# Four modulation groups of the second layer, moved from the first layer's mixers to the end of its experts

## The chip, the cores and the metric

The kernel runs on one core of one Trainium2 chip. The metric is the device time of one execution in microseconds; three runs of the kernel before are shown. The engines are named as the profile names them: PE (matmul; PEld is its weight load), DVE (vector), ACT (scalar), POOL (GpSimd) and SP (the sync engine, which here issues nearly all DMAs; its rows read SPq).

## What is computed

Two layers of a transformer trunk over 512 latent and 256 context tokens of 1024 values. In each layer a vector of six modulations, made of a conditioning vector and a weight, scales and shifts the normed tokens; four token mixers run side by side (a gated recurrence HGRN2, neighbourhood attention, a gated linear attention, latent attention); an output projection follows, and then a mixture of 32 experts with two experts for each token. Cut to what matters here:

```python
for layer in range(DEPTH):
    m_lat = jnp.split((c_act @ w_mod[layer] + b_mod[layer])[:, None, :], 6, axis=-1)
    m_ctx = jnp.split(c_ctx_act @ w_mod[layer] + b_mod[layer], 6, axis=-1)
    h = rmsnorm(x, norm1_g[layer]) * (1.0 + m_lat[1]) + m_lat[0]
    hc = rmsnorm(xc, norm1_g[layer]) * (1.0 + m_ctx[1]) + m_ctx[0]
    p = split_projection(h @ w_in[layer])
    ...
    x = x + m_lat[5] * y[b * l_ctx:].reshape(b, n, D_MODEL)
```

`w_mod[layer]` is 1024 x 6144. The kernel cuts its columns into 12 groups of 512. Groups 0 to 3 are `m[0]` and `m[1]`, the shift and scale of the first norm; a layer needs them at its very start. They depend on nothing that the layer before computes.

## The kernel before, in words

**Modulation.** `modulation` (L323) is a generator; one step makes one group. It loads the bias into one of four small tiles `bmt` (L329, two DMAs), loads the weight in two DMAs of 1 MB into ring tiles (L334), runs 32 matmuls on PE with the 32-column conditioning `cT` as the stationary side (L336, recorded at the helper's line L294; the trace has two instructions for each), adds the bias on DVE into `mr` (L338), and for groups 0 to 3 turns the result on PE (L340) and copies it into `ABs`, the scale and shift of the first norm (L341, L346).

**The last mixers of a layer** (L1424). `weave` (L428) takes steps from three generators so that their progress stays in proportion to the numbers in `STEPS` (L38): HGRN2 (66), latent attention (72), and `mods` (12 in the first layer, 8 in the second). In the first layer `mods` makes groups 4 to 11 of its own layer and then groups 0 to 3 of the next (L1419 to L1422). The weights of `mods` go through a ring of two tiles (L1413). The profile's first layer has this stage from about 345 to 506 us.

**Experts.** For each of 16 pairs of experts six pieces of 1 MB are loaded (128 + 64 DMAs in both layers, L1453 and L1458) into 18 slots that `wslot` (L1441) hands out in turn, so that a piece reuses the slot of the piece 18 before it, that is, of the third pair before. Each load also waits until the load four before it has landed (`DEEP`, L34). Pair `p_` runs on PE: up (L1917), activation, down (L1939); DVE weights the result, and POOL adds it to the stream `XA` in DRAM with an indirect DMA (`scatter`, L1992). A run-time branch (L2018) adds work for pairs with many tokens. After the pairs stands one more branch (L2032) for the rare case of many tokens left; it is not taken here. Its other arm waits, on SP, for every DMA that SP has issued, and on PE for PE's own work; only behind it stand the instructions of the next layer. The first layer's experts run from about 620 to 921 us.

**Start of the next layer.** SP loads 0.5 MB of `w_in` in three DMAs of short rows (L514) and then six token tiles `xn` from `XA` (L463), which wait for the last scatter. ACT splits the weight (L519) and squares each `xn` (L471), DVE scales it (L479), PE turns it (L490), ACT applies `ABs` (L497), and the projections begin.

**What sets the order.** Each engine runs its instructions in one fixed order, made at build time by a scheduler from the order of the code, with loads moved ahead where only a free tile holds them back. Semaphores hold an instruction until its inputs and its tile are free; whatever stands behind a waiting instruction on its engine waits too.

Of the kernel before, what the change touches and what calls it, by code (L numbers as in the profile page):

```python
# [17 lines left out]
P = 128  # L18
# [7 lines left out]
NEXP = 32  # L26
# [8 lines left out]
YE = 3  # L35
PRE = 2

STEPS = ((38, 24, 60, 18, 12, 12, 66, 72, 12), (38, 24, 60, 18, 12, 12, 66, 72, 8))  # L38
NWM = 4
NU, NX, NM = 25, 8, 8  # L40
TOKS = ((256, 512), (0, 256))
# [45 lines left out]
def hybrid_kernel(ctx: ExitStack, tc: tile.TileContext, a: dict, out: bass.AP, dbg=None, stop=None):  # L87
    nc = tc.nc
# [79 lines left out]
    def pmd():  # L168
        return psum("md")[:, 0:P]
# [123 lines left out]
    def mm(o, lhsT, rhs, start, stop, **kw):  # L293
        TE.matmul(o, lhsT, rhs, start=start, stop=stop, **kw)  # L294
# [24 lines left out]
    bmt = [cp.tile([P, P], F32, name=f"bmt{i}") for i in range(4)]  # L319
    for t_ in bmt:  # L320
        V.memset(t_, 0.0)

    def modulation(L, gs, slot=None, bank=None):  # L323

        for i_, g in enumerate(gs):
            cs = slice(g * 512, (g + 1) * 512)
            bt = bmt[i_ % 4]
            for w in range(2):
                nc.sync.dma_start(bt.rearrange("(j r) c -> j r c", r=32)[:, w, :], a["b_mod"][L, cs].rearrange("(j c) -> j c", j=4))  # L329
            pm = bank()[:, 0:P] if bank else pmd()  # L330
            for k in range(KT):
                if k % 4 == 0:
                    wt = (slot or ring)([P, 4, 512])
                    nc.sync.dma_start(wt, a["w_mod"][L, k * P:(k + 4) * P, cs].rearrange("(k p) c -> p k c", p=P))  # L334
                for j in range(4):
                    mm(pm[32 * j:32 * j + 32, 0:P], cT[:, k, :], wt[:, k % 4, j * P:(j + 1) * P], k == 0, k == KT - 1)  # L336
            mr = cp.tile([P, P], F32, name="mr", tag="mr", bufs=2)
            V.tensor_tensor(mr, pm[:, 0:P], bt, op=ALU.add)  # L338
            if g < 4:
                TE.transpose(pm[:, 0:P], mr, ident)  # L340
                V.tensor_copy(ABs[L][:, :, g // 2, 4 * (g % 2):4 * (g % 2) + 4],  # L341
                              pm[:, 0:P].rearrange("p (j c) -> p c j", j=4)[:, 0:2, :])
            if g in (2, 3):
                ks = slice(4 * g - 8, 4 * g - 4)
                for w in range(2):
                    V.scalar_tensor_tensor(ABs[L][:, w, 1, ks], ABs[L][:, w, 1, ks], 1.0, g1s[:, L, ks], op0=ALU.add, op1=ALU.mult)  # L346
            if g in (8, 9):
                g2 = cp.tile([P, P], F32, name="g2", tag="g2", bufs=1)
                V.memset(g2, 0.0)
                for w in range(2):  # L350
                    nc.sync.dma_start(g2.rearrange("(j r) c -> j r c", r=32)[:, w, :],
                                      a["norm2_g"][L, (g - 8) * 512:(g - 7) * 512].rearrange("(j c) -> j c", j=4))
                V.scalar_tensor_tensor(mr, mr, 1.0, g2, op0=ALU.add, op1=ALU.mult)
            if 6 <= g < 10:
                TE.transpose(pm[:, 0:P], mr, ident)
                V.tensor_copy(AB2s[L][:, :, g // 2 - 3, 4 * (g % 2):4 * (g % 2) + 4],
                              pm[:, 0:P].rearrange("p (j c) -> p c j", j=4)[:, 0:2, :])
            if g >= 4:
                for w in range(2):
                    nc.sync.dma_start(MOD[L][w, cs].rearrange("(j c) -> j c", j=4),  # L360
                                      mr.rearrange("(j r) c -> j r c", r=32)[:, w, :])
            yield
# [18 lines left out]
    def layer(L):  # L381
        last = L == DEPTH - 1
# [40 lines left out]
        def drain(*gens):  # L423
            for g_ in gens:
                for _ in g_:
                    pass

        def weave(*gens):  # L428

            st_ = [[g_, 0, n_] for g_, n_ in gens]  # L430
            while st_:
                s_ = min(st_, key=lambda e_: e_[1] / e_[2])
                try:
                    next(s_[0])
                    s_[1] += 1
                except StopIteration:
                    st_.remove(s_)
# [454 lines left out]
        def gla_values(E, gv):  # L892
            wt = wchunk([(C_G + 256, 256)], not E.safe)
            gv.extend(v_tiles(E))
            yield from tm(E, wt, 0, 256, lambda p, n: S.copy(gv[n], p), range(NT))
# [504 lines left out]
        nq, nk, nv, hq, hg, gg, zz, gs, hv, gqk, gv, cs, mw, mr_ = ([] for _ in range(14))  # L1400
        gqk.extend((gq, gk))
        drain(gla_values(Ex, gv))
        st = STEPS[L]
        weave((gla(E, gqk, gv, c2, False), st[0]),
# [13 lines left out]

        def mods():  # L1419
            yield from modulation(L, range(4, 12))  # L1420
            if not last:
                yield from modulation(L + 1, range(4))  # L1422

        weave((hgrn_, st[6]),  # L1424
              (chain(mla_qkv(Em, hu, cs, c2, mw, mr_), restore(Ex), mla(Em, mr_)), st[7]), (mods(), st[8]))
# [13 lines left out]
        NW = sum(SLOTS[L])  # L1439

        def wslot():  # L1441
            i = pieces[0] % NW
            pieces[0] += 1
            for p_, n_ in slots:
                if i < n_:
                    return wpools[p_].tile([P, 2048], F32, name=f"w{p_}", tag=f"w{p_}", bufs=n_ + XGS * (p_ == 2))
                i -= n_
# [21 lines left out]
        def prefetch(n, order=True, after=None):  # L1469

            for _ in range(n):
                e, i = len(loaded) // 6 + NEXP // 2 * (len(loaded) % 2), len(loaded) % 6 // 2
                if len(loaded) < 3 * NEXP:
                    loaded.append(expert_part(wgu[e], wdn[e], i, order, after, True))
# [19 lines left out]
        def split_chunk(raw):  # L1494
            hi = ring([P, 4, 256], F32R)
            S.activation(hi, raw, AF.Copy)
            lo = ring([P, 4, 256], F32R)
            V.tensor_tensor(lo, raw, hi.bitcast(F32), op=ALU.subtract)  # L1498
            return hi, lo
# [7 lines left out]
        wt = split_chunk(raw)  # L1507
# [151 lines left out]
        for c in range(4):  # L1659
# [3 lines left out]
            for kh in range(2):  # L1663
                if (c, kh) != (0, 0):
                    wt = split_chunk(raw)
# [168 lines left out]
        def rows(p_):  # L1834
            if p_ < NEXP // 2:
                return gather(xgs[p_ % NG], tab(0, p_, "row"))
# [9 lines left out]
        def tab(b, p_, n_):  # L1846
            return tabs[b][n_][:, p_:p_ + 1] if n_ in tabs[b] else None
# [54 lines left out]
        def block_in(xg, xT=None):  # L1902
# [8 lines left out]
                (V.tensor_copy if g else S.copy)(xT[:, 4 * g:4 * g + 4], pt.rearrange("p (k t) -> p k t", k=4))  # L1911
            return xT

        def span(hv):
            return slice(64 * hv[0], 64 * hv[-1] + 64)

        def block_up(w_, xT, hv=(0, 1)):  # L1917

            pm = pmm()
            for k in range(KT):  # L1920
                for h in hv:
                    hs = span([h])
                    mm(pm[hs, :], xT[:, k, hs], w_[h][k // 4][:, k % 4, :], k == 0, k == KT - 1)
            ac = wk.tile([P, 256], F32, name="ac", tag="ac", bufs=1)
            rs_ = span(hv)
            S.activation(ac[rs_], pm[rs_, 0:256], AF.Silu)  # L1926
            V.tensor_tensor(ac[rs_], ac[rs_], pm[rs_, 256:512], op=ALU.mult)  # L1927
            return ac
# [63 lines left out]
        def scatter(ye, row):  # L1992


            G.indirect_dma_start(out=XA, out_offset=bass.IndirectOffsetOnAxis(ap=row, axis=0), in_=ye, in_offset=None,  # L1995
                                 bounds_check=T - 1, oob_is_err=False, compute_op=ALU.add)
# [3 lines left out]
        def pair(p_):  # L2000
            return [loaded[6 * p_ + h:6 * p_ + 6:2] for h in range(2)] if p_ >= 0 else None
# [6 lines left out]
        xT = into(0)  # L2008
        for p_ in range(NP):
            prefetch(max(0, min(6 * p_ + NW, 3 * NEXP) - len(loaded)), False)  # L2010
            w_ = pair(p_)
            xT_, ac = xT, block_up(w_, xT)
            rows(p_ + NG)
            if p_ + 1 < NP:
                xT = into(p_ + 1)
            gt = gates_of(tab(0, p_, "own"))
            ye = weighted(p_, block_down(w_, block_act(ac)), gt, tab(0, p_, "gws"))
            with tc.If(cregs[p_] > 0):  # L2018
                with tc.If(cregs[p_] < 2) as c1_:
                    half_swapped(p_, w_[0], xT_, ye, gt, 1)  # L2020
                with c1_.Else():
                    with tc.If(cregs[p_] < 3) as c2_:
                        half_swapped(p_, w_[1], xT_, ye, gt, 0)
                    with c2_.Else():
                        swapped(p_, w_, xT_, ye, gt)

                        gather(yes[:, (p_ + 2) % YE], tab(1, p_, "row"))
                        y1 = block_down(w_, block_act(block_up(w_, into(p_, 1, xT_))))
                        scatter(weighted(p_ + 1, y1, gates_of(tab(1, p_, "own")), tab(1, p_, "gws")), tab(1, p_, "row"))
            scatter(ye, tab(0, p_, "row"))  # L2030

        with tc.If(cregs[NP] > 64):  # L2032
            for b in range(2, 12):
# [87 lines left out]
```

## Time and profile before

| what | value |
| --- | --- |
| three runs, median (lowest to highest) | 1757.4 us (1752.9 to 1762.54) |
| profiled execution, own time | 1761.22 us |
| its span, first to last instruction | 1759.4 us |
| mean granted PE clock | 0.933 |
| PE busy, whole span | 1463.9 us (83%) |
| DVE, ACT, POOL busy | 711.2, 525.2, 348.3 us |
| loads of `w_mod` in the ring | 40 of 1 MB |
| loads of expert weights | 192 of 1 MB |
| moved by all DMA engines | 366.01 MB |

The profile cuts the span into 40 slices of 44 us and gives busy shares in tenths. Whole-span shares mix stages of different limits, so the stretches around the change are read one by one: the last mixers of the first layer, the end of its experts, and the first 30 us of the second layer.

### The profile page before, as it was taken

The page shows a single profiled execution, that of the slowest core. Times are in us where ns is not written, and L with a number is a line of the kernel's source. Part 1 is how long each engine was busy: PE and PEld are TensorE (multiplying, and loading weights), DVE is VectorE, ACT ScalarE, POOL GpSimd, SP SyncE. Part 2 cuts the span into 40 slices and gives each one's busy share as a digit, 9 for nine tenths or more (in the row PEclk, how much of TensorE's full clock was granted, in tenths as well). Part 3 has the DMA queues.
Part 4 walks back from the last instruction along what each step waited for, and adds up shares of the span by engine and source line. Part 5 has one row for each costly group of instructions (what it writes and reads, how often), then busy time and mean ns, then how long its engine had stood idle before and what let it go on. Part 6 is the DMA issues. An engine that isn't in the chain of part 4 may idle for free. (4 is left out here: it accounts for less than half of the span.)

```text
span 1759.4 us, 26653 instructions
## 1 busy us (share of the span) xinstructions
PE 1463.9 (83%) x10515; PEld 986.2 (56%) x10515; DVE 711.2 (40%) x1427; ACT 525.2 (30%) x1067; POOL 348.3 (20%) x263
## 2 busy tenths in 40 slices
PE   6999999989889748887876999897887866888883
PEld 4888778746679723322236888685455852322221
DVE  5263353586733552111125443626874262111111
ACT  5342453464422101100006433626543211000001
POOL 0021120120101333645330120302110131111100
PEclk9999989999999869999997999899898888999997
DMA  9232311167447299999974333104343659999995
GB/s 329 88 110 75 115 56 34 39 226 239 160 159 214 107 393 354 383 372 383 375 274 130 107 101 90 31 31 134 109 140 128 187 183 382 378 361 364 374 387 220
DMA packets 179800, 366.01 MB, mean 208 GB/s; under 512 B 39608, under 2 KB 90496, under 8 KB 179328
## 3 DMA queue, kind: packets, MB, share of 16 engines
q1 hardware_dynamic: 170288, 342.10, 54.8%
q0 software_dynamic: 9216, 20.99, 4.7%
q8 instruction: 138, 2.26, 0.5%
q14 instruction: 78, 0.64, 0.1%
q10 hardware_dynamic: 80, 0.02, 0.0%
HBM read 338.48 MB, written 39.65 MB: 215 GB/s over the span
## 5 line engine op out<-in xcount | busy, mean ns | idle before, releaser
L294 PE MATMUL mm<-w,xT 128*64 128x512 f32 (+1 forms) x1120 | 273.4, 597 | 34.8 <-DMA w<-in_moe_w_gu_dram 16.3
L294 PE MATMUL pj<-h,w 128*128 128x256 f32 (+1 forms) x1224 | 228.0, 341 | 0.5 <-DVE u L935 0.3
L294 PEld LDWEIGHTS pj<-h,w 128*128 128x128 f32 x1224 | 189.5, 191 | 29.1 <-issue 5.2
L294 PEld LDWEIGHTS mm<-w,xT 128*64 128x64 f32 x1120 | 88.3, 141 | 192.0 <-issue 137.6
L294 PE MATMUL sc<-w,aT 128*64 128x512 f32 x536 | 138.4, 607 | 19.3 <-ACT aT L1936 16.7
L294 PE MATMUL pj<-w,h 128*128 128x256 f32 x864 | 117.3, 293 | 0.0
L1995 POOL DMA_INDIRECT XA<-yes,row x32 | 50.8, 1588 | 330.7 <-DVEq L2018 278.8
L294 PEld LDWEIGHTS pj<-w,h 128*128 128x128 f32 x864 | 110.3, 198 | 3.6 <-issue 3.0
L1927 DVE TENSOR_TENSOR ac<-ac,mm 128x256 f32<-128x256 f32 x32 | 13.5, 421 | 243.6 <-ACT ac L1926 243.5
L1926 ACT ACTIVATE ac<-mm 128x256 f32<-128x256 f32 x32 | 12.3, 384 | 318.0 <-PE mm L294 318.0
L294 PEld LDWEIGHTS sc<-w,aT 128*64 128x64 f32 x536 | 44.7, 138 | 90.1 <-issue 55.9
L294 PE MATMUL mm<-w,h 128*128 128x256 f32 x624 | 84.4, 296 | 10.7 <-PEq L1514 5.4
L521 DVE TENSOR_TENSOR w<-w 128x2048 fp32r<-128x2048 f32 (+1 forms) x26 | 58.0, 2229 | 81.2 <-ACT w L519 81.2
L294 PEld LDWEIGHTS mm<-w,h 128*128 128x128 f32 x624 | 81.1, 203 | 11.2 <-issue 5.7
L1610 POOL TENSOR_TENSOR xh<-xc,gr 128x512 f32<-128x512 f32 (+1 forms) x25 | 30.9, 1240 | 195.9 <-DVE xc L1608 135.0
L294 PE MATMUL sc<-h 128*128 128x256 f32 (+3 forms) x144 | 60.4, 537 | 11.0 <-ACT um L1211 10.2
L1910 PEld LDWEIGHTS pt<-masks,w 128*128 128x128 f32 x256 | 28.3, 146 | 66.1 <-issue 54.0
L519 ACT ACTIVATE w<-w 128x2048 fp32r<-128x2048 f32 (+1 forms) x26 | 48.0, 1847 | 51.9 <-PE pj L294 37.2
L294 PE MATMUL x<-u 64*32 64x32 f32 (+5 forms) x944 | 55.2, 254 | 8.5 <-DVE u L775 8.2
L1911 ACT COPY xT<-pt 128x512 f32<-128x512 f32 x32 | 18.7, 586 | 142.8 <-PE pt L1910 108.5
L1910 PE MATMUL pt<-masks,w 128*128 128x128 f32 x256 | 40.8, 291 | 24.5 <-DMA w<-XG,row 13.5
L294 PE MATMUL sc<-h,w 128*128 128x512 f32 (+1 forms) x312 | 59.4, 350 | 0.3 <-ACT ux L297 0.3
(397 smaller groups left out, 2410.2 us busy)
## 6 DMA issues: line engine op xcount, KB each, us to landing
w<-in_moe_w_gu_dram SPq DMA_DIRECT2D x128, 1024.0 KB
w<-in_moe_w_dn_dram SPq DMA_DIRECT2D x64, 1024.0 KB
w<-in_w_mod_dram SPq DMA_DIRECT2D x40, 1024.0 KB
w<-in_w_in_dram SPq DMA_DIRECT2D x22, 1024.0 KB
wm<-in_w_mod_dram SPq DMA_DIRECT2D x8, 1024.0 KB
XG<-xg SPq DMA_DIRECT2D x10, 512.0 KB
w<-in_w_out_dram SPq DMA_DIRECT2D x8, 512.0 KB
w<-in_w_out_dram SPq DMA_DIRECT2D x16, 256.0 KB
```

The source lines that it names most:

```text
L294: TE.matmul(o, lhsT, rhs, start=start, stop=stop, **kw)
L519: S.activation(hi[:, :, 0:o], raw[:, :, 0:o], AF.Copy)
L521: V.tensor_tensor(lo[:, :, 0:o], raw[:, :, 0:o], hi[:, :, 0:o].bitcast(F32), op=ALU.subtract)
L1610: G.tensor_tensor(xh[:, t0 - qt0:t0 - qt0 + m, cs], xs, bc(gr[:, 1, w], 0, m), op=ALU.mult)
L1910: TE.transpose(pt[:, u * P:(u + 1) * P], xg[:, o:o + P], ident)
L1911: (V.tensor_copy if g else S.copy)(xT[:, 4 * g:4 * g + 4], pt.rearrange("p (k t) -> p k t", k=4))
L1926: S.activation(ac[rs_], pm[rs_, 0:256], AF.Silu)
L1927: V.tensor_tensor(ac[rs_], ac[rs_], pm[rs_, 256:512], op=ALU.mult)
L1995: G.indirect_dma_start(out=XA, out_offset=bass.IndirectOffsetOnAxis(ap=row, axis=0), in_=ye, in_offset=None, bounds_check=T - 1, oob_is_er ...
```

## The change

The four groups 0 to 3 of the second layer leave the mixers of the first. Their weights are loaded into expert slots behind the last expert pieces, from the point where the third pair before has given its slots back (groups 0 to 2 in the iteration of pair 14, group 3 in that of pair 15), and without the limit of four loads in flight. Their matmuls stand on PE behind the last pair and ahead of the branch at the end. `STEPS` of the first layer counts 8 steps of `mods` in place of 12. Groups of the mixers' own layer stay where they were made, and the second layer has nothing moved.

```diff
-STEPS = ((38, 24, 60, 18, 12, 12, 66, 72, 12), (38, 24, 60, 18, 12, 12, 66, 72, 8))
+STEPS = ((38, 24, 60, 18, 12, 12, 66, 72, 8), (38, 24, 60, 18, 12, 12, 66, 72, 8))
...
+    def mod_bias(L, g, bt):
+        for w in range(2):
+            nc.sync.dma_start(bt.rearrange("(j r) c -> j r c", r=32)[:, w, :],
+                              a["b_mod"][L, g * 512:(g + 1) * 512].rearrange("(j c) -> j c", j=4))
+
+    def mod_weights(L, g, kh, wt):
+        nc.sync.dma_start(wt, a["w_mod"][L, kh * 512:(kh + 1) * 512, g * 512:(g + 1) * 512].rearrange("(k p) c -> p k c", p=P))
...
-    def modulation(L, gs, slot=None, bank=None):
+    def modulation(L, gs, slot=None, bank=None, there=None):
...
             for k in range(KT):
                 if k % 4 == 0:
-                    wt = (slot or ring)([P, 4, 512])
-                    nc.sync.dma_start(wt, a["w_mod"][L, k * P:(k + 4) * P, cs].rearrange("(k p) c -> p k c", p=P))
+                    if there:
+                        wt = there[g][k // 4]
+                    else:
+                        wt = (slot or ring)([P, 4, 512])
+                        mod_weights(L, g, k // 4, wt)
...
         def mods():
             yield from modulation(L, range(4, 12))
-            if not last:
-                yield from modulation(L + 1, range(4))
...
+        ahead = {}
+
+        def mod_ahead(g):
+            mod_bias(L + 1, g, bmt[g])
+            ahead[g] = [wslot().rearrange("p (k c) -> p k c", k=4) for _ in range(2)]
+            for kh in range(2):
+                mod_weights(L + 1, g, kh, ahead[g][kh])
...
         for p_ in range(NP):
             prefetch(max(0, min(6 * p_ + NW, 3 * NEXP) - len(loaded)), False)
+            for g in () if last else range(4):
+                if g not in ahead and 6 * p_ + NW >= 3 * NEXP + 2 * g + 2:
+                    mod_ahead(g)
...
             scatter(ye, tab(0, p_, "row"))
+        if not last:
+            for _ in modulation(L + 1, range(4), None, pmm, ahead):
+                pass
```

**PE, end of the last mixers of the first layer.** A group's matmuls read `x<-w,cT`, 32 of them, in one row or two. Before (from the row in which the check of the recurrence's range, `fmax`, is turned):

```order
L1395 MATMUL x<-masks,fmax 1x128
...
L294 MATMUL x<-w,cT 32x128 x32
L966 MATMUL x<-masks,um 128x128 x4
L340 MATMUL x<-masks,mr 128x128
...
L294 MATMUL x<-w,cT 32x128 x32
L294 MATMUL x<-u 128x128
L966 MATMUL x<-masks,um 128x128 x2
L340 MATMUL x<-masks,mr 128x128
```

and with the change, over the same stretch of the recurrence:

```order
L1406 MATMUL x<-masks,fmax 1x128
...
L294 MATMUL x<-w,cT 32x128 x5
L294 MATMUL x<-um 64x128 x12
L294 MATMUL x<-w,cT 32x128 x27
L294 MATMUL sc<-h 128x256
```

Two groups stood behind `fmax`, each with a turn of `mr`; one is left there, and it is a group of the first layer. In the whole stage 12 groups became 8, spread over the same steps of the two mixers.

**SP, from the last expert load to the second layer.** Names ending in numbers are buffers; the waits in brackets are semaphores of DMAs (DMAHW for SP's eight lanes, DMASW for POOL's DMAs) and of engines. Before:

```order
L1458 DMA w2_15415<-in_moe_w_dn_dram 128x2x1024 [waits DMAHW3_49,PE_49]
L1458 DMA w2_15417<-in_moe_w_dn_dram 128x2x1024 [waits DMAHW4_49]
...
L2032 COMPARE_AND_BRANCH
...
L2032 UNCONDITIONAL_BRANCH [waits DMAHW0_49,DMAHW1_49,DMAHW2_49,DMAHW3_49,DMAHW4_49,DMAHW5_49,DMAHW6_49,DMAHW7_49]
L514 DMA w_17186<-in_w_in_dram 128x8x64 [waits DMAHW1_49,PE_49]
...
L463 DMA xn0_17220<-XA_104 128x1024 [waits DMASW7_49,DMAHW4_49,DMASW3_49,PE_49]
```

and with the change:

```order
L1467 DMA w2_15241<-in_moe_w_dn_dram 128x2x1024 [waits DMAHW4_49]
L329 DMA w2_15466<-in_w_mod_dram 128x4x512 [waits PE_49]
...
L329 DMA w2_15706<-in_w_mod_dram 128x4x512 [waits DMAHW0_49]
L325 DMA bmt0_151<-in_b_mod_dram 4x128 [waits DMAHW1_49,DVE_49]
...
L325 DMA bmt3_154<-in_b_mod_dram 4x128 [waits DMAHW7_49,DVE_49]
L2056 COMPARE_AND_BRANCH
...
L2056 UNCONDITIONAL_BRANCH [waits DMAHW0_49,DMAHW1_49,DMAHW2_49,DMAHW3_49,DMAHW4_49,DMAHW5_49,DMAHW6_49,DMAHW7_49]
L525 DMA w_17186<-in_w_in_dram 128x8x64 [waits DMAHW1_49,DMAHW0_49,PE_49]
...
L474 DMA xn0_17220<-XA_104 128x1024 [waits DMAHW3_49,DMASW7_49,DMASW3_49]
```

Eight loads of `w_mod` and seven bias loads now stand between the last expert piece and the branch. The bias loads are not those of the moved groups (these were hoisted into the mixers): they are the second layer's own first ones, for groups 4 to 7, into the same four tiles `bmt`, so each waits for the DVE addition of a moved group that reads the tile. Before, their place was in the mixers.

**DVE, the same place,** with the change; the first row is group 0's addition, the last is group 3's, and each waits for its matmuls:

```order
L349 TENSOR_TENSOR mr_15950<-mm_15917,bmt0_151 128x128 [waits PE_49]
...
L349 TENSOR_TENSOR mr_16063<-mm_16030,bmt3_154 128x128 [waits PE_49]
```

The last bias load of SP waits for that last row, which is new here.

## Rows read from the trace of the kernel before

**Rows 1.** The page's 40 slices of 44 us: busy tenths of PE and of the DMA engines.

```profile
PE   6999999989889748887876999897887866888883
...
DMA  9232311167447299999974333104343659999995
```

**Rows 2.** Stretches of 20 us: length, busy us and instructions by engine, granted clock, DMA share, GB/s.

```profile
420.00:440.00 20.00, 19.48 (x261) 15.26 (x249) 9.25 (x26) 7.72 (x20) 0.00 (x0) 1.00 0.62 215
440.00:460.00 20.00, 14.22 (x209) 9.79 (x210) 19.40 (x35) 9.87 (x25) 2.04 (x2) 0.99 0.64 209
460.00:480.00 20.00, 19.70 (x271) 14.27 (x273) 10.80 (x26) 7.32 (x17) 5.62 (x5) 0.92 0.32 111
480.00:500.00 20.00, 19.12 (x268) 14.69 (x256) 8.68 (x26) 8.46 (x19) 0.00 (x0) 1.00 0.36 127
...
880.00:900.00 20.00, 16.81 (x75) 6.15 (x76) 3.03 (x5) 2.10 (x5) 6.86 (x3) 1.00 1.02 388
900.00:920.00 20.00, 17.09 (x97) 7.70 (x94) 5.17 (x8) 1.98 (x5) 6.85 (x3) 1.00 0.67 206
920.00:940.00 20.00, 2.56 (x12) 1.47 (x8) 5.09 (x7) 8.05 (x13) 1.59 (x1) 0.60 0.65 202
```

**Rows 3.** Finer stretches, same columns (PE, PEld, DVE, ACT, POOL, clock, DMA, GB/s).

```profile
12.00:20.00 8.00, 7.32 (x30) 5.28 (x31) 6.31 (x15) 6.91 (x23) 0.00 (x0) 1.00 1.05 389
896.00:902.00 6.00, 5.16 (x30) 2.84 (x32) 1.77 (x3) 0.37 (x1) 0.00 (x0) 1.00 1.02 413
902.00:908.00 6.00, 4.55 (x36) 2.62 (x32) 0.42 (x1) 0.64 (x2) 0.00 (x0) 1.00 0.88 351
...
914.00:920.00 6.00, 4.54 (x23) 1.65 (x20) 0.60 (x2) 0.76 (x2) 4.63 (x2) 1.00 0.90 166
922.00:928.00 6.00, 0.00 (x0) 0.00 (x0) 1.50 (x2) 1.06 (x1) 1.34 (x1) 0.66 0.49 72
...
938.00:944.00 6.00, 5.05 (x23) 4.08 (x23) 5.07 (x10) 6.00 (x13) 0.00 (x0) 0.50 0.81 284
```

**Rows 4.** SP's DMA issues in order of time: start, us, line, tile, count.

```profile
881.34 2.86 SPq L1458 DMA_DIRECT2D w<-in_moe_w_dn_dram  x2
...
899.01 2.88 SPq L1458 DMA_DIRECT2D w<-in_moe_w_dn_dram  x2
912.33 1.85 SPq L514 DMA_DIRECT2D w<-in_w_in_dram  x3
929.07 0.81 SPq L463 DMA_DIRECT2D xn<-XA  x2
```

**Rows 5.** All engines in order of time at the boundary of the layers; idle time before in brackets.

```profile
916.92 3.70 PE L294 MATMUL sc<-w,aT 128*64 128x512 f32 x16 [0.52 <-ACT aT L1936]
...
921.75 1.59 POOL L1995 DMA_INDIRECT XA<-yes,row  x1 [3.04 <-DVEq L2018]
925.66 1.06 ACT L519 ACTIVATE w<-w 128x1024 fp32r<-128x1024 f32 x1 [8.79 <-PEq L2032]
...
932.95 1.06 ACT L471 ACTIVATE junk<-xn 128x1024 f32<-128x1024 f32 x1 [6.23 <-DMA xn<-XA]
```

**Rows 6.** Instructions that read `cT`, by stretch: length, PE, PEld and DVE busy.

```profile
480.00:500.00 20.00, 3.18 (x112) 2.64 (x100) 0.00 (x0) 1.00 0.36 127
...
sum 200.00, PE 25.91 PEld 20.47 DVE 0.00; mean PE 2.59 PEld 2.05 DVE 0.00
```

**Rows 7.** PE in order of time, moved groups among the mixers.

```profile
457.04 0.33 PE L340 MATMUL x<-masks,mr 128*128 128x128 f32 x1 [1.39 <-DVE mr L338]
...
479.27 1.95 PE L294 MATMUL x<-w,cT 128*32 128x128 f32 x64
```

**Rows 8.** PE's waits from 340 to 510 us: total, times, longest.

```profile
PE x L294 <- DMA w<-in_w_mod_dram: 3.7, 4, 2.1
```

**Rows 9.** PE in order of time: half a group, in the first layer's mixers.

```profile
355.41 1.08 PE L294 MATMUL x<-w,cT 128*32 128x128 f32 x32 [2.08 <-DMA w<-in_w_mod_dram]
```

**Rows 10.** PE in order of time at the kernel's start: the turn behind a group.

```profile
25.55 0.33 PE L340 MATMUL pt<-masks,mr 128*128 128x128 f32 x1 [0.41 <-DVE mr L338]
```

More of the change, by code (lines that the diff above doesn't have):

```diff
@@ L327, in modulation @@
             bt = bmt[i_ % 4]
-            for w in range(2):
-                nc.sync.dma_start(bt.rearrange("(j r) c -> j r c", r=32)[:, w, :], a["b_mod"][L, cs].rearrange("(j c) -> j c", j=4))
+            if not there:
+                mod_bias(L, g, bt)
             pm = bank()[:, 0:P] if bank else pmd()
```

## The prediction

> **What bounds the kernel now.** I read the page's 40 slices first, then stretches around the two places that the change touches, then SP's issues and the boundary of the layers in order of time. The slices [rows 1] show PE at 9 tenths or near it in most of the mixers, the DMA engines at 9 through the experts (slices 15 to 20 for the first layer), and near 920 us both leaving: that is the seam between the layers.
>
> In the last mixers [rows 2] PE is busy 38.8 of the 40 us from 460 to 500 while the DMA engines carry a share of 0.32 to 0.36. So there PE sets the pace, and work taken off PE shortens the stage. From 440 to 460 it does not: PE is busy 14.2 of 20 us and DVE 19.4.
>
> At the end of the experts it is the other way round. From 896 to 902 us the DMA share is 1.02 at 413 GB/s, and it is still 0.88 from 902 to 908 [rows 3]; the last two expert loads are issued from 899.01 to 901.9 [rows 4]. Then SP stands until 912.33, when it issues the first loads of the second layer, `w_in` [rows 4]. Its arm of the branch waits for its eight DMA lanes alone, so 912.33 says when the last straggler of the expert loads had been reported; PE is at work on the last pair until 916.92 + 3.70 = 920.6 [rows 5].
>
> From there the path is: last scatter issued by POOL at 921.75, `xn` loads issued at 929.07, first square on ACT at 932.95, whose idle time is ended by that load [rows 5]. From 922 to 928 PE does nothing [rows 3]. This hole of some 12 us on PE (920.6 to 932.95) is one in which four groups of matmuls would cost nothing. The question is whether their weights are there in time.
>
> **The change, part by part.**
>
> *Taken from the mixers.* The 200 us sum of instructions that read `cT` has PE at 25.91 us for twelve groups [rows 6], 2.16 a group (1.95 at its best [rows 7]); four make 8.6. Each also has a turn of 0.33 us, before one of which PE waits 1.39 us for DVE's `mr` [rows 7]. DMA waits of these matmuls come to 3.7 us in the whole stage [rows 8], some of it those of the first groups, which stay. Everything: 8.6 + 4 x 0.33 + up to 1.39 + 3.7 = 15, which no stage gives back whole. In the new order the stretch from `fmax` on has one group fewer in the part from 460 to 500, and two more are missing earlier, some of them beside DVE's full stretch from 440 to 460. I take 7 us: 0.97 of three groups at 2.5 each (2.16 + 0.33), the 0.97 being PE's 38.8 of 40 us, and next to nothing for the fourth. Bounds: 3 (only the one group that leaves the PE-bound part counts, and its turn) and 11 (all four, and the 1.39).
>
> *Added behind the experts: 8 loads of 1 MB.* They stand on SP behind the last expert piece and wait for slots of pair 13, and of pair 14 for the last group; PE has left these by then, since pair 15 is at its end at 920.6. So DMA bandwidth is their limit. 8 x 1.049 = 8.39 MB at 389 GB/s, the rate from 12 to 20 us, where loads of the same rows of `w_mod` run [rows 3], take 21.6 us. Two scatters fall among them. What one costs the loads: six pieces of a pair take 17.67 us (881.34 to 899.01 [rows 4]), six pieces alone at 413 GB/s 6 x 1.049/0.413 = 15.2, the rest is 2.44; two make 4.9. Without a straggler, expert traffic ends at about 902 + 0.88 x 6 = 907.3, with it at 912.33. So the last weight lands at 907.3 + 21.6 + 4.9 = 933.8, or at 938.8 with a tail of 5 us like the one before. I take 937, since SP waits for the last straggler of every load.
>
> The Trainium skill, "DMA: Bandwidth & Descriptors", Specifications, gives about 358 GB/s as the limit of the memory for one core; an estimate by it makes the eight loads 23.4 us and the sum 1.9 us larger. The rows do not agree (389 and 413 GB/s), and the rows decide.
>
> *Added on SP: the arm of the branch now waits for these loads, and for seven small ones.* The seven bias loads ahead of the branch reuse tiles that the moved groups read, and the last waits for DVE's addition of group 3. So the chain behind the last landing is: half a group on PE, 1.08 us [rows 9]; the addition, 0.41 us with its wait [rows 10]; issue of the bias load at 1.85/3 = 0.6 us [rows 4]; its landing, 929.07 to 932.95 = 3.9 us [rows 4, 5] less the 1.3 us that the 0.5 MB of `xn` take at about 400 GB/s, so 2.6; 0.3 for the branch itself. Sum 5.0, so `w_in` is issued at 942.0 where it was 912.33. Its issue takes 1.85, and `xn` goes out at 943.9 (before: 929.07). It then lands after 3.9 us, plus what `w_in` ahead of it in the same queue costs: two stretches of 6 us, of which one carries `w_in` and one does not (shares 0.90 and 0.49 [rows 3]), differ by 2.5 us of all engines' time, of which some 1.9 are over by `xn`'s issue, so 0.6. First square at 948.4 against 932.95: **15.5 us later**.
>
> Bounds: with the last landing at 933.8 it is +12.3. With 938.8 it is +17.3, and with half a group at half the clock (1.08 more) and 0.2 more of `w_in`, +18.6. What the end hides anyway: the last scatter lands before (issue 921.75, free by 929; some 3 us later under load), and PE's gate (the last group 2 us behind its weights, then 5.0 us from PE's end to ACT's first instruction as before, 920.6 to 925.66 [rows 5]) gives 944, ahead of the square. The DVE additions and copies, 8 instructions under 0.6 us each, lie in ACT's and DVE's idle time. The four biases of the moved groups go ahead early and cost nothing where no one waits.
>
> *Second layer behind the square.* It runs as it did; its own groups 4 to 7 find their biases loaded earlier, which no row shows PE waiting for. Zero.
>
> *Sum.* -7 + 15.5 = **+8.5 us**, with -11 + 12.3 = +1 and -3 + 18.6 = +16 as its ends. The profiled execution took 1761.22 us (span 1759.4); it would take 1769.7. It stands 3.8 us above the median of the three runs, 1757.4, to which I add the same term: **1766**.
>
> **The rivals.**
>
> *Rival A, faster: the hole takes it all.* The seam has 21.8 us from 907.3 to `xn`'s issue with the DMA engines at 0.65 to 0.67 [rows 2]. If the weights land early enough, nothing is added, and 7 us go: 1750, with the gain's upper end 1746. It decides at the landing: `xn` keeps 929.07 only if `w_in` goes out by 927.2, so if the chain of 5.0 us starts by 922.2, 14.9 us behind 907.3. That asks for 563 GB/s; the highest row has 413. It holds if the loads overtake expert pieces or SP's arm does not wait for what I say. Against it stands 912.33, long before PE's end: SP waited there, and for loads.
>
> *Rival B, slower still: the mixers give nothing back.* DVE is full from 440 to 460 [rows 2], and if the recurrence's chain of DVE, PE and ACT and not PE's load sets the length, PE's freed time turns into waits. The gain is then 2 us or less: -2 + 15.5, 1771. For it: PE at 14.2 of 20 in that stretch. Against it: 38.8 of 40 behind it.
>
> *Rival C, the clock gives some back.* In 938 to 944 us, the second layer's first matmuls, the granted clock is 0.50 (the 1.2 GHz level) with PE busy 5.05 of 6 us, behind a hole in which it fell to 0.60 to 0.66 [rows 2, 3]. With the moved matmuls in the hole, PE's idle stretch before the layer is some 8 us in place of 12, and if it keeps 2.4 GHz, about half of those 5.05 us and some of what follows, 3 us, come back: 1763. Against it: the groups wait for their weights, so PE idles between them too.
>
> The Trainium skill, "TensorE: Matmul & The Clock Gate", Loop structure matters more than you think, counts just such matmuls, with a wait for a DMA between them, as the ones that run at the lower clock; by it rival C fails and the chain's half group costs the 1.1 us of my upper end. No row of the kernel before shows groups that wait so in this place, and pair 15 with its waits for loads held 1.00 [rows 3].
>
> **How the numbers follow.** A measurement of this kernel tells 0.5%, 8.8 us, from no change. The forecast has 0.70: its centre lies just inside that bound, so 0.36 of it counts as same and 0.34 as slower. Rival A has 0.10 (0.06 beyond the bound, 0.04 within), rival B 0.12 (slower), rival C 0.08 (0.06 same, 0.02 slower). Faster 0.06, same 0.46, slower 0.48. The range goes from +1 with rival C's 3 taken off and 2 for a median of three runs that lie 9.6 us apart, 1753, to the forecast's upper end of +16 with the same 2, and 1 more for rival B with a late landing, 1776. It leaves out rival A and little else.
>
> **What would show it.** Right: in the profile after, SP issues the first `w_in` some 30 us later than before against the end of the expert traffic, and behind bias loads that wait for DVE; PE waits for `w_mod` behind pair 15; the first square comes some 15 us later against the last expert matmul; the stage of the last mixers is about 7 us shorter. Wrong: `xn` is issued as soon after the last scatter as before (then A); the mixers are less than 3 us shorter (B); the clock from the first square on is 1.00 (C); or the time between the last expert matmul and the first square grows by far more or less than 15, and then the step on the landing at 937 is the one that failed.

## The result, and the profile after

| | median us | runs | ratio to before | 95% interval |
| --- | --- | --- | --- | --- |
| before | 1757.67 | 5 | | |
| the change | 1771.65 | 5 | 1.0083 | 1.0061 to 1.0106 |
| before, third set of runs | 1758.65 | 31 | | |
| the change, third set | 1772.83 | 11 | 1.0069 | 1.0042 to 1.0096 |

The kernel became slower by 14.0 us, where the forecast was 8.5 us slower (1766 in a range of 1753 to 1776). The profiled execution has a span of 1771.7 us against 1759.4, so +12.3, and these 12.3 us can be laid out along the program. Two lengths are used from here on. The **mixers' stretch** goes from the first matmul of a modulation group in that stage to the first load of expert weights. The **seam** goes from the end of the last expert matmul on PE to the first square on ACT.

PE of the changed kernel in order of time, the start of the last mixers:

```profile
352.14 1.94 PE L294 MATMUL x<-w,cT 128*32 128x128 f32 x32 [2.28 <-DMA w<-in_w_mod_dram]
```

and SP, the first loads of expert weights, of the kernel before and then of the changed one:

```profile
503.73 6.29 SPq L1453 DMA_DIRECT2D w<-in_moe_w_gu_dram  x2
```

```profile
491.84 5.62 SPq L1462 DMA_DIRECT2D w<-in_moe_w_gu_dram  x2
```

The mixers' stretch was 503.73 - 355.41 = 148.3 us [rows 9] and is 491.84 - 352.14 = 139.7: 8.6 us shorter. PE's own time for the groups fell by less:

```profile
352.00:492.00 140.00, 20.00 (x512) 15.14 (x512) 0.00 (x0) 0.95 0.42 140
```

(PE's busy time is the second number after the stretch: 20.00 where twelve groups had 25.91 [rows 6].) All of PE's work in the two stretches, of the kernel before and then of the changed one:

```profile
355.41:503.73 148.32, 132.38 (x1705) 90.84 (x1705) 104.53 (x211) 70.76 (x160) 22.23 (x15) 0.98 0.57 189
```

```profile
352.14:491.84 139.70, 125.14 (x1445) 85.39 (x1445) 103.33 (x199) 70.24 (x159) 22.39 (x15) 0.95 0.42 139
```

PE's busy time fell by 7.2 us: 5.9 for the groups and 1.3 for four turns of 0.33. All its waits together came to 17.3 us before and 16.5 with the change, so the waits hardly count.

Now the seam. SP's issues, answering to [rows 4]:

```profile
892.59 21.94 SPq L329 DMA_DIRECT2D w<-in_w_mod_dram  x8
923.53 9.07 SPq L325 DMA_DIRECT2D bmt<-in_b_mod_dram  x7
936.25 2.67 SPq L525 DMA_DIRECT2D w<-in_w_in_dram  x3
939.05 1.15 SPq L474 DMA_DIRECT2D xn<-XA  x2
```

PE in order of time, idle time before in brackets:

```profile
910.00 3.70 PE L294 MATMUL sc<-w,aT 128*64 128x512 f32 x16 [0.52 <-ACT aT L1954]
915.48 1.14 PE L294 MATMUL mm<-w,cT 128*32 128x128 f32 x33 [1.77 <-PEq L2039]
921.22 1.93 PE L294 MATMUL mm<-w,cT 128*32 128x128 f32 x31 [4.60 <-issue]
...
923.97 2.49 PE L294 MATMUL mm<-w,cT 128*32 128x128 f32 x64
...
932.13 0.33 PE L351 MATMUL mm<-masks,mr 128*128 128x128 f32 x1 [0.41 <-DVE mr L349]
948.44 1.94 PE L501 MATMUL mm<-masks,xn 128*128 128x128 f32 x8 [15.98 <-DVE xn L490]
```

and ACT, answering to [rows 5]:

```profile
941.67 1.06 ACT L530 ACTIVATE w<-w 128x1024 fp32r<-128x1024 f32 x1 [31.72 <-DMA w<-in_w_in_dram]
943.62 1.06 ACT L482 ACTIVATE junk<-xn 128x1024 f32<-128x1024 f32 x1 [0.89 <-DMA xn<-XA]
```

The last expert matmul ends at 913.70 where it ended at 920.62, the first square stands at 943.62 where it stood at 932.95: the seam grew from 12.3 to 29.9 us, by 17.6. What SP waited for ahead of `w_in` in its last stretch (total, times, longest):

```profile
SPq L525 <- PEq L2056: 2.3, 1, 2.3
SPq L325 <- DVE mr L349: 1.5, 1, 1.5
```

The line that ends the chain is the first: `w_in` (L525) is released by PE's sequencer at the branch (L2056), not by a DMA lane. SP had nothing else to wait for from about 933.9 on, 2.3 us before. The whole span in parts: -3.3 ahead of the mixers' first group (352.14 against 355.41; nothing is changed there), -8.6 in the mixers, -0.1 from there to the first expert matmul, +5.1 in the pairs of experts (283.6 us against 278.5), +17.6 in the seam, +1.6 behind it. That is +12.3. The two large terms are the change; whether the 5.1 us of the pairs belong to it had to be seen.

### The profile page after: what moved, and what is told of

Same layout as the page of the kernel before. It is cut to its first block, busy times and chain, and to the rows that moved or that the text cites. A ratio compares the mean times of both kernels' runs of the same rounds, so it can differ in the third digit from the quotient of the medians.

```text
span 1771.7 us, 26637 instructions
## 1 busy us (share of the span) xinstructions
PE 1470.2 (83%) x10515; PEld 990.7 (56%) x10515; DVE 712.8 (40%) x1427; ACT 524.8 (30%) x1067; POOL 348.7 (20%) x263
## 5 line engine op out<-in xcount | busy, mean ns | idle before, releaser
L1944 ACT ACTIVATE ac<-mm 128x256 f32<-128x256 f32 x32 | 12.3, 383 | 317.6 <-PE mm L294 317.6
L294 PE MATMUL sc<-h 128*128 128x256 f32 (+3 forms) x144 | 61.0, 542 | 13.3 <-ACT um L1222 12.6
L1619 POOL TENSOR_TENSOR xh<-xc,gr 128x512 f32<-128x512 f32 (+1 forms) x25 | 31.1, 1247 | 195.1 <-DVE xc L1617 143.6
```

Source lines behind the costliest of these rows:

```text
L1619: G.tensor_tensor(xh[:, t0 - qt0:t0 - qt0 + m, cs], xs, bc(gr[:, 1, w], 0, m), op=ALU.mult)
```

## The experiments

Lengths in us from one profile each. "Pairs" goes from the first to the last expert matmul of the first layer. Ratios are to the kernel before on the same chips. Executions of one kernel lie up to 13 us apart and more (the change, third set: 1764.4 to 1777.1). From the first square to the end the profiles take 819 to 828 us, the two of the change 828 and 822; the two that lie outside are named below. So a few us between two rows mean nothing by themselves.

| kernel | groups in mixers | mixers | pairs | seam | ratio (95% interval) |
| --- | --- | --- | --- | --- | --- |
| before | 12 | 148.3 | 278.5 | 12.3 | |
| the change | 8 | 139.7 | 283.6 | 29.9 | 1.0083 (1.0061 to 1.0106) |
| the change again | 8 | 140.6 | 280.4 | 31.9 | 1.0069 (1.0042 to 1.0096) |
| bias loads later | 8 | 141.9 | 279.1 | 30.8 | 1.0037 (1.0020 to 1.0054) |
| left out | 8 | 140.9 | 277.7 | 11.6 | not comparable |
| both places | 12 | 148.9 | 279.1 | 32.0 | 1.0120 (1.0092 to 1.0147) |
| loads alone | 12 | 151.8 | 277.7 | 23.5 | 1.0063 (1.0046 to 1.0080) |
| matmuls behind the branch | 8 | 139.9 | 283.5 | 19.4 | 1.0035 (1.0014 to 1.0055) |
| two groups, matmuls behind | 10 | 143.6 | 278.0 | 13.1 | 0.9984 (0.9962 to 1.0006) |
| the same again | 10 | 143.8 | 280.1 | 13.3 | 0.9981 (0.9960 to 1.0002) |
| two groups, loads behind too | 10 | 144.3 | 278.7 | 16.3 | 0.9984 (0.9966 to 1.0001) |
| three groups, matmuls behind | 9 | 142.9 | 298.5 | 13.0 | 1.0086 (1.0057 to 1.0116) |
| three groups, filled | 10 | 143.3 | 279.8 | 16.3 | 1.0113 (1.0075 to 1.0152) |

**Bias loads later.** My chain for the seam ended in SP's bias loads, which wait for DVE's addition of the last moved group. This kernel takes them away from there:

```diff
+            if L == 1 and g >= 4:
+                tc.keep_in_program_order(ins)
```

> The seam is counted from the end of the last expert matmul on PE to the first square on ACT: 12.3 us before, 29.9 us with the change. This kernel is the change, except that the second layer's own bias loads are kept behind the branch. Theory (SP's arm waits for the landings and then for bias loads that hang on DVE's addition of the last moved group): w_in goes out about 0.7 us behind the last landing of w_mod, which stands 14.9 us behind the last expert matmul, so xn at 18.4 and the square at 23; PE's gate (moved groups end at 18.8, and 5.0 from there to ACT's first instruction) puts it at 24 to 25. Seam 23 to 25, time 1765 to 1767. Rival (the landing of 8 MB alone sets the seam, the bias loads hang on nothing that is late): seam 30, time 1771.

The seam stayed: 30.8. So the bias loads were not the last gate. SP's waits around the seam, and its `w_in`:

```profile
SPq L2058 <- SPq L2058: 14.1, 1, 14.1
...
SPq L527 <- PEq L2058: 5.4, 1, 5.4
```

```profile
897.61 21.85 SPq L331 DMA_DIRECT2D w<-in_w_mod_dram  x8
939.73 2.94 SPq L527 DMA_DIRECT2D w<-in_w_in_dram  x3
```

The arm waits 14.1 us for the lanes, until about 919.46 + 14.1 = 933.6, 17.5 behind the last expert matmul (916.05). Then `w_in` waits 5.4 us more, for PE. PE's last turn of a moved group:

```profile
935.52 0.33 PE L353 MATMUL mm<-masks,mr 128*128 128x128 f32 x1 [0.41 <-DVE mr L351]
```

It ends at 935.85, and `w_in` goes out 3.9 us behind it. In the change the same distance is 932.46 to 936.25, 3.8; in the change's second profile 4.1, with both places 3.8. It is the same with the bias loads and without. The rival on record came closer in number (30), but not in its reason: the landing was over 6 us earlier. The kernel is nearer to before than the change is (1.0037, about +6.5 us), though its mixers, pairs and seam are about as long. Behind the square its profile takes 820.5 us, which one profile cannot tell from chance; why it is faster stays open.

**Both places, and loads alone.** In the first, the mixers keep twelve groups and the four are loaded and computed again behind the experts. In the second, the eight loads are there, nothing reads them, and the moved groups' bias loads are left out.

```diff
-STEPS = ((38, 24, 60, 18, 12, 12, 66, 72, 8),
+STEPS = ((38, 24, 60, 18, 12, 12, 66, 72, 12),
...
+            if not last:
+                yield from modulation(L + 1, range(4))
```

> The mixers keep their twelve groups, and the four are loaded and computed a second time behind the experts, as in the change: the added half alone. Theory: the mixers are as before, the seam is 30 as with the change, time 1757.7 + 17.6 = 1775. Also: PE again stands 4 to 5 us behind its first half group, with no wait that the profile names, if that is a matter of loading its code and not of a weight. Rival (the experts' end was at an unlucky phase in the profile of the change, and the added half costs less when it starts elsewhere): seam under 25, time 1770 or less.

> The mixers keep their twelve groups; the eight loads stand behind the experts and nothing reads them, so neither matmuls nor additions nor waiting bias loads are there. Theory: SP's arm still waits for the landings, 15 us behind the last expert matmul; here xn stands ahead of w_in in SP's order, so it goes out at 16 and the square follows 4 to 5 us later. Seam 20 to 21, time 1766. Rival (PE and the bias loads make all of the cost, the landings none): seam 12 to 13, time 1758.

Both places: seam 32.0, ratio 1.0120, which is 21 us on 1761.79 where the seam gives 19.7; the theory's 1775 was too low, since this set's kernel before was slower too. PE stood again, here behind 27 matmul instructions:

```profile
919.70 1.03 PE L294 MATMUL mm<-w,cT 128*32 128x128 f32 x27 [1.85 <-PEq L2041]
925.43 2.35 PE L294 MATMUL mm<-w,cT 128*32 128x128 f32 x37 [4.69 <-issue]
```

Loads alone: seam 23.5, with SP waiting 15.6 us in the arm and `xn` going out at 942.43, 19.7 behind the last expert matmul (922.70). So the landings alone make 11 us of the seam in this kernel, and those that also have the matmuls ahead of the branch have another 6.4 to 8.5 us. The split is rough, since the landing differs by profile (the same eight loads cost 7 us in a kernel below), and here `xn` stands ahead of `w_in` on SP. Neither theory (20 to 21) nor rival (12 to 13) had the size.

**Left out.** The second layer's four groups are made nowhere.

> The kernel before without the second layer's four groups anywhere: the second layer uses the first layer's scale and shift. Nothing is added behind the experts. Theory (PE sets the pace of the last mixers): the mixers are 8 to 9 us shorter (8.7 in the two profiles), the seam stays 12.3, time 1749. Rival 1 (the recurrence sets the pace there): 1757. Rival 2 (the experts give back part of what the mixers gain, as they did in the profile of the change, where 12.1 us of lead at their start were 6.9 at their end): 1752 to 1754.

Up to the seam this is the gain without the cost: mixers 140.9, pairs 277.7, seam 11.6. The rival that the pairs give back what the mixers gain falls. Its total says nothing on the change: the second layer works on other values, and took 868 us from the square to the end, where before and the change took 826 and 828.

**The change again, and matmuls behind the branch.** If PE's passing of the branch holds `w_in`, the matmuls must stand behind the branch. The loads stay where they are; in this kernel and all that follow, the second layer's own bias loads stand behind the branch too.

```diff
-        if not last:
-            for _ in modulation(L + 1, range(4), None, pmm, ahead):
-                pass
...
         with tc.If(cregs[NP] > 64):
...
+        if not last:
+            for _ in modulation(L + 1, range(4), None, pmm, ahead):
+                pass
```

> The change itself once more, beside the kernels of this set and the same runs of before. Seam 30 as in its first profile; the mixers 8.8 us shorter (mean of three profiles with eight groups there, 140.9 us from the first mod matmul to the first expert load, against 149.7 with twelve); so 17.6 - 8.8 = +9 us over before if the experts' stage scatters by chance alone (+4.5 in the first profile), +14 if the change really slows that stage.

> The change with the four groups' matmuls behind the branch, and the second layer's own bias loads kept behind it too; the eight loads stand where they stood. Theory (PE's passing of the branch, some 4 us behind the last moved group, releases w_in, and that sets the seam): PE passes early, SP goes on with the landings at 15 to 15.6 behind the last expert matmul, xn goes out and the square follows 4 us later. Seam 20, up to 23.5 if the landings are as late as in the kernel with loads alone; 6.5 to 10 us faster than the change, before -1 to +3. Rival (PE is not the gate, the landings are): seam 30 and the change's time.

The change repeats: seam 31.9, +12.1 us by its ratio, which does not exclude the +9 nor the +14. Its pairs took 280.4, so the 5.1 us of the first profile are not a property of the change that these runs show; the kernel with the matmuls behind has the same loads and 283.5.

Behind the branch the seam is 19.4 us, 10.5 to 12.5 shorter. SP, PE and ACT of that kernel:

```profile
927.51 2.26 SPq L476 DMA_DIRECT2D xn<-XA  x5
929.88 7.75 SPq L527 DMA_DIRECT2D w<-in_w_in_dram  x3
```

```profile
908.14 3.70 PE L294 MATMUL sc<-w,aT 128*64 128x512 f32 x16 [0.52 <-ACT aT L1956]
921.42 4.45 PE L294 MATMUL mm<-w,cT 128*32 128x128 f32 x74 [9.58 <-PEq L2055]
...
942.54 0.79 PE L294 MATMUL pj<-h,w 128*128 128x256 f32 x2 [0.47 <-ACT w L532]
```

```profile
931.27 1.06 ACT L484 ACTIVATE junk<-xn 128x1024 f32<-128x1024 f32 x1 [23.18 <-PE mm L353]
```

`xn` goes out 15.7 us behind the last expert matmul (911.84), as the landings have it, and PE computes the groups beside SP and the DMAs. So PE's gate is gone. Two things went together here, the matmuls ahead of the branch and the order on SP, where five `xn` now stand ahead of `w_in`; they were not tried apart. The time gained less than the seam: 1.0035 is +6 us, where 19.4 - 12.3 - 9.1 = -2. Of that 2.5 us can be seen: `w_in` is now behind five `xn`, and the first projection starts at 942.54, 30.7 behind the last expert matmul, 9.6 later than before (941.70 - 920.62 = 21.1), where the square is 7.1 later. The profiled execution, 1760.04 us, is also the second fastest of twelve (median 1764.3). The rest stays open, and with it how much of a seam reaches the time: the kernel with the bias loads later has the same ratio in another set (1.0037) with a seam 11.4 us longer.

**Two groups.** The landings are the second gate, so fewer loads should vanish behind the last scatter. Two groups move, with their matmuls behind the branch; once more on another chip; and with the loads behind the branch too.

```diff
+STEPS = ((38, 24, 60, 18, 12, 12, 66, 72, 10),
...
+            if not last:
+                yield from modulation(L + 1, range(2))
...
+            for g in () if last else range(2, 4):
```

> As before, with two groups moved (10 steps). Theory: four loads land before the last scatter does, seam 12.3 to 13, the mixers give 4.4; before -3.5 to -4.5. Rival (each load adds its time): seam 12.3 + 4 x 2.6 = 22.7, before +6.

> The kernel with two groups moved and their matmuls behind the branch once more, since its ratio of 0.9984 had an interval that includes 1. Theory (the sum of seam +0.7 and mixers -4.4): before -3.5. Rival (nothing is left of it): before 0.

> Two groups moved with matmuls behind the branch, and their four loads behind it as well, ahead of xn on SP. Theory: SP passes the branch when the expert loads have landed, some 8 us ahead of the last expert matmul; the four loads (10.6 us, one scatter of 2.4, 2 us to the first byte) end 7 us behind it, xn waits for the last scatter as before: seam 12.3 to 14, mixers -4.4, before -3 to -4. Rival (xn is queued behind the weights): seam 16 and before 0.

The seam is 13.1 and 13.3, and `xn` waits for the last scatter as it did before the change:

```profile
SPq L2057 <- SPq L2057: 14.1, 1, 14.1
SPq L476 <- DMA XA<-yes,row: 3.6, 2, 2.8
```

The mixers of the three kernels are 5.8 us shorter than the mean of those with twelve groups (149.7). Ratios 0.9984 and 0.9981, about 3 us: each interval just reaches 1, both sets point the same way. It is the best kernel here and no proven gain. With the loads behind the branch the ratio is the same 0.9984, and the seam is 16.3. That is the rival's number, but not its reason (`xn` queued behind the weights). SP's waits there:

```profile
SPq L476 <- DMA XA<-yes,row: 15.3, 2, 14.5
...
SPq L527 <- PE mm L294: 2.6, 1, 2.6
```

`xn` goes out at 929.98, 12.5 us behind the last expert matmul (917.53), because it waits for the last scatter, and it lands 3.8 us later, as before (3.9). The scatter is what took longer: 11.3 us from its issue (918.66) to that of `xn`, where it was 7.3 before [rows 4, 5], with the DMA engines at a share of 1.04 to 1.06 from 917 to 922. The second line bears on PE's gate. Behind the branch, `w_in` waits for the moved groups' matmuls themselves and goes out at 933.53, where the last of them ends at 933.47. So `w_in` seems to be loaded where the moved weights lay, and what the change made late may be that place and not the branch as such. A kernel with the moved weights elsewhere was not run.

**Three groups, and a strange stretch.**

> As the kernel with the matmuls behind the branch, but three groups are moved and the first stays in the mixers (9 steps). Theory: the sixth load lands 7.2 us behind the last expert matmul (profile of the change), xn waits for the last scatter anyway (issue 8.5 behind it in the kernel before), so the seam is 13 to 15; the mixers give 6.6; before -4 to -6. Rival (any load behind the experts adds its 2.6 us to the seam): seam 12.3 + 6 x 2.6 = 28, before +9.

The seam is 13.0, as the theory has it, but the pairs took 298.5 us, and the kernel is slower by 0.86%. PE's waits from 636 to 915 us of this kernel (the branches of the pairs, ahead of the first transposes and the first matmuls):

```profile
PE pt L1923 <- PEq L2043: 22.5, 8, 3.3
PE mm L294 <- PEq L2043: 6.5, 2, 3.3
```

and of the kernel with two groups, same code there:

```profile
PE pt L1923 <- PEq L2043: 8.5, 9, 1.8
PE mm L294 <- PEq L2043: 5.9, 3, 2.1
```

The next kernel makes the first group twice in the mixers, loads and matmuls, so that PE's program ahead of the experts is as long as with two groups moved.

```diff
-                yield from modulation(L + 1, range(1))
+                yield from modulation(L + 1, (0, 0))
```

> Three groups moved as before, and the first group's 32 matmuls made twice in the mixers, so that PE's program ahead of the experts is as long as with two groups moved. With three groups moved the stretch from the first to the last expert matmul was 298.6 us where six other profiles have 278 to 284, and PE waited 22.5 us for its own branches ahead of the pairs' first transposes, where the others have 8.2 to 11.4. Theory (the length of the code ahead shifts where the branches of the pairs fall in what is loaded of PE's program): the stretch is 278 to 284 again, those waits 8 to 11, the seam 13; time 20 - 2 = 18 us under the kernel with three groups, before -2. Rival (the six loads in expert slots slow the pairs): 298 again.

The first layer's pairs are back at 279.8, and their waits are lower than in any other kernel. But the time stayed, 1.0113: the second layer's pairs, 1455 to 1790 us, now wait:

```profile
PE pt L1923 <- PEq L2043: 4.6, 8, 1.8
PE mm L294 <- PEq L2043: 4.5, 3, 1.8
...
PE pt L1923 <- PEq L2043: 19.7, 8, 3.8
PE mm L294 <- PEq L2043: 7.0, 3, 3.5
```

(The first two lines are the first layer, the last two the second, where eight other profiles have 2.5 to 4.3 in the third line's place.) From the square to the end this profile takes 841 us. So these waits moved from one layer to the other with an edit that only adds code ahead of the experts. That the length of the code decides it rests on these two kernels, and what the waits consist of is not shown. The seam of 16.3 here, with the same six loads, leaves three groups without a fair trial.

## Why the prediction was right, and where it was not

**Sign and place: right.** The forecast said that the mixers pay back less than the seam costs, and that the cost stands where `w_in` and `xn` wait on SP. With the mixers' gain (mean of the profiles with twelve groups, 149.7, less the mean of the five with eight, 140.6) of 9.1 us, and a seam 17.6 to 19.6 longer, the sum is +8.5 to +10.5. The forecast's +8.5 had the same two terms, both too small: 7 and 15.5. The measured +14.0 and +12.1 leave 1.6 to 5.5 us that no row assigns; the second interval (+7.4 to +16.9) includes the sum, the first (+10.7 to +18.6) just misses it.

**The mixers: 9.1 for 7.** I counted three of four groups. All four count: in the mean of the same profiles PE is busy 125.1 us in the stretch where it was 134.1, 8.9 less, and its waits stay at 17. Two groups gave 5.8. DVE's full stretch from 440 to 460 [rows 2] did not hold the others back, so rival B fell.

**The landing: right within 3.3 us.** I had it at 937, 16.4 behind the last expert matmul. In the change the DMA engines carry next to nothing from 929 on, 15.3 behind it. With the bias loads later SP's arm ends at 17.5; `xn` goes out at 15.7 with the matmuls behind the branch and at 19.7 with the loads alone. One of the loads did wait for its slot, 2.6 us for PE, where I had taken PE to have left all of them.

**The chain behind the landing: wrong.** This is the step that failed: "PE's gate (the last group 2 us behind its weights, then 5.0 us from PE's end to ACT's first instruction as before [...]) gives 944, ahead of the square". Two things were wrong in it. PE was not 2 us behind the weights: it made one half group, stood 4.6 us, and then ran three and a half groups in a row, 921.22 to 932.46, some of it at the lower clock. It never waited for `w_mod` there, which I had named as a sign of being right. And it is not only ACT that hangs on PE's passing of the branch: the order on record shows a PE semaphore among the waits of `w_in`, which I read as a free tile that PE would long have left. In the kernel before it was one: `w_in` went out at 912.33 [rows 4], while PE was still at work ahead of the branch. Now `w_in` goes out when PE has passed the branch, 3.8 to 4.1 us behind the last moved group in four profiles, and `xn` is queued behind `w_in`. The bias loads that I priced in its place cost the seam nothing (30.8 without them). Their chain was there all the same, and ended only 2.3 us ahead of PE's gate; its 0.3 us for the branch had no row, and SP's own waits at the branch come to 0.7 us in the change. That a forecast by the wrong gate came so near is luck: forecast seam 27.8, measured 29.9 and 31.9.

**The clock.** The upper bound had an extra for half the clock on the last half group. The half clock came, but on the half group behind PE's stand, while the last one ran at 1.00: stretches of the change, length, busy times by engine, granted clock, DMA share and GB/s.

```profile
913.00:917.00 4.00, 1.85 (x37) 1.01 (x34) 1.41 (x2) 0.00 (x0) 1.38 (x1) 1.00 1.03 389
917.00:921.00 4.00, 0.00 (x0) 0.00 (x0) 0.00 (x0) 0.00 (x0) 0.21 (x1) 0.66 1.06 373
921.00:923.00 2.00, 1.78 (x31) 1.46 (x30) 0.00 (x0) 0.00 (x0) 0.00 (x0) 0.50 1.05 269
...
929.00:931.00 2.00, 1.58 (x52) 1.38 (x51) 0.69 (x4) 0.00 (x0) 0.00 (x0) 1.00 0.00 1
...
948.40:954.40 6.00, 4.83 (x20) 3.90 (x21) 4.90 (x9) 6.00 (x12) 0.00 (x0) 0.50 0.71 257
```

PE idles from 917 to 921, and the matmuls behind run at 0.50, the 1.2 GHz level: 31 in 1.93 us, where 32 took 1.08 [rows 9]. The Trainium skill, "TensorE: Matmul & The Clock Gate", Loop structure matters more than you think, says that matmuls with a long wait for a DMA between them run at the lower clock. The trace agrees on the clock (0.50), though it names no DMA for this wait. The second layer's first matmuls are at 0.50 as before [rows 3], so rival C fell. Rival A fell with the seam.

## What to carry to other kernels

Work that is moved ahead of a run-time branch can hold what stands behind the branch and waits for its engine, DMA issues included (`w_in` here, 3.8 to 4.1 us behind PE's last work): look in the order for semaphores of that engine on the first loads behind, and try the work behind the branch if its result is needed late. In a hole between two stages count what can land before the wait that ends it anyway; here four loads ahead of the branch fit (seam +0.8 to +1.0) and eight did not (+7 to +11 without matmuls ahead of the branch). Where the wait is for a scatter, loads behind the branch can make that scatter itself late (seam +4.0). A group that leaves a full engine gives back what the engine was busy with, and no waits: the stage lost 9.1 us for 8.9 us of PE's busy time.

## What was not expected of the hardware

PE stood 4.3 to 4.7 us behind the first 27 to 33 matmul instructions of the moved groups in all four profiles that have them ahead of the branch, with no wait that the profile names ("issue"), while the DMA engines were full. In the profile with 27 it stands short of the 32 that read the first weight, so it is no wait for the second. In 917 to 921.2 us of the change one packet of instructions was moved (queue q8), but so was one from 910 to 917 and one from 921.2 to 926. That the wait is one for code behind the weights in the queues is possible; it was not tried.

```profile
DMA packets 759, 1.56 MB, mean 372 GB/s; under 512 B 32, under 2 KB 32, under 8 KB 757
...
q8 instruction: 1, 0.02, 1.6%
```

And PE waited 8 to 11 us at the pairs' branches, ahead of the first transposes, in the first layer of most kernels, 4.6 at best and 22.5 at worst. In the second layer of one kernel it was 19.7, 15 to 17 us more than in eight others. Between the kernels with 22.5 and with 4.6 only one group more is made in the mixers. The two are slower than before by 0.9 and 1.1%; what sets these waits is open.
